# Causal mask by selects, a stream of row maxima and a scaled split of w_out in a transformer layer

## The chip, the cores and the metric

The kernel runs on one core of one Trainium2 chip. The metric is device time in microseconds (us) of one execution, lower being better. The chip's engines are named TensorE (PE), VectorE (DVE), ScalarE (ACT), GpSimd (POOL) and SyncE (SP, which issues most of the DMAs). PEld is TensorE's weight load, which runs beside the matmuls.

## What is computed

One layer for 2048 tokens of width 1024: a token mixer of eight attention heads with forget gates beside a chunked spatial gating unit, one output projection, then a SwiGLU feed-forward block (FFN). The part that the change touches is the attention and what feeds it:

```python
xn = rms_norm(x, mix_norm_g)
q, k, v, f_logit, z = split(xn @ w_in)
c = cumsum(log_sigmoid(f_logit + b_f))          # per head, along the tokens
s = einsum('bqhd,bkhd->bhqk', q, k) * Dh ** -0.5
s = s + c[t] - c[s]
s = where(key_pos <= q_pos, s, -inf)            # causal
p = softmax(s)
attn = einsum('bhqk,bkhd->bqhd', p, v)
...
merged = concatenate([rms_norm(attn, g_a), rms_norm(sgu, g_s)])
x = x + merged @ w_out
```

## The kernel before

All matrix products are made from fp32 numbers that are split in two parts, high and low; a product is three matmuls (high by high, high by low, low by high). `hi_of` casts the high part, `lo_of` subtracts it from the number for the low one; both are helpers, so their instructions carry L102 and L107 wherever they are called.

**Stage 1 (0 to 360 us).** Four chunks of 512 tokens. Each chunk makes the forget gates' rows, q and k, then v, and in between works off pieces of three side jobs through `between`: the rows of the forget gates (`forget_rows`), the next chunk's normalisation and split (`Chunk.steps`), and the row maxima of the previous chunk (`early_max`). A row maximum is the bound that exp subtracts; it needs a product q k of its own with high parts alone (`one_max`, one matmul of up to 512 columns and one reduction on VectorE, 128 queries by 512 keys each), a split of the result (`max_split`) and a transposition (`max_rows`). Everything that the attention reads (QH, QL, KH, KL, VD, XS, the gates' rows AUG) is stored to DRAM through SP's queue. In chunk 0, v is made first, in four PSUM banks that are closed (`v_close`) into normalised tiles after the weights of q have been split.

**Stage 2 (360 to 1011 us).** Attention, over 32 units (head h, chunk of queries j), each of 4j+4 steps of 128 keys: 320 steps. A step is `qk`: two matmuls into PSUM (L624, L625), on the last four steps of a unit, the diagonal blocks, a third (L627) that adds -1e30 above the diagonal by a product of the identity with a mask; then exp on ScalarE into Pt (L629), its cast Ph on ScalarE and its low part Pl on VectorE. Two steps later follows `pv_of`: three matmuls with Ph and Pl (L640 to L642). Between the steps come pieces of the z projections and of the spatial gating (`gates`, up to step 293), of `prep` (loads of the keys two units ahead, and, for the heads and chunks that stage 1 has not covered, their row maxima in one run of 4(j+1) matmuls), and from step 276 on of `out_weights`: w_out is loaded, multiplied by the output gain on GpSimd (`gain`, L799), cast on ScalarE and subtracted on GpSimd. From step 300 on the output tiles follow.

**Stage 3 (1011 to 2511 us).** The FFN; the change doesn't touch it.

Which instruction of an engine comes first is set by a scheduler when the kernel is built: it follows the order of the program, save that an instruction may move ahead of others that are not ready by its model of the engines. Each engine then runs its own list strictly in order, and SP's list of DMAs too. A wait for one tile so holds everything behind it on that engine.

## Time and profile before

| | us |
|---|---|
| median of 3 runs | 2509.7 |
| lowest, highest | 2504.14, 2510.0 |
| profiled execution | 2512.58 |
| its span | 2510.8 |
| TensorE busy | 2437.3 |
| VectorE busy | 1562.2 |
| ScalarE busy | 1054.5 |
| GpSimd busy | 555.6 |

The durations of the profile come from the one profiled execution. Its time has some 1.8 us around the span, and lies 2.9 us above the median of the runs. The busy shares are averages over stages that are unlike, so the profile is read by stretches: a window's row gives each engine's busy time with its number of instructions, and the granted TensorE clock as a share of the full one. Matmuls are pipelined: their records overlap, and the distance from one start to the next, not the length of a record, is what one costs.

### The profile page before, as it was taken

Reading aid. Unit: us, or ns where it says so; the run is one execution under the profiler, and the core shown is the slowest. Engines: PE = TensorE matmul, PEld = TensorE weight load, DVE = VectorE, ACT = ScalarE, POOL = GpSimd, SP = SyncE. Lnnn points to the kernel's source line nnn. Section 1 sums busy time; section 2 is a strip of 40 time slices with the busy share of each in tenths; the row PEclk is TensorE's granted clock in tenths of the full one; section 3 lists DMA queues with packets and bytes.
Section 4 is the critical chain, followed back from the end, with each engine's and each line's share of the span. In section 5 each row is a group of like instructions: output and inputs, shape, how many; then the busy total and the mean of one; then the engine's idle time right before and its main releaser. Section 6 shows DMA issues by size and latency. Waiting matters only on the chain. (4 is left out here: it accounts for less than half of the span.)

```text
span 2510.8 us, 31035 instructions
## 1 busy us (share of the span) xinstructions
PE 2437.3 (97%) x10857; PEld 1949.1 (78%) x10857; DVE 1562.2 (62%) x2537; ACT 1054.5 (42%) x1787; POOL 555.6 (22%) x442
## 2 busy tenths in 40 slices
PE   7899999999999989999999999999999999999998
PEld 5677777787777776877788888878888877888876
DVE  4457485555456666455755555775555587586887
ACT  4312236667777666333423333433232342232333
POOL 1000000000000024122223323233232234454441
PEclk9999999999999988999999999999999999999999
DMA  9766574334433336665422232342322335455454
GB/s 307 259 223 207 162 210 131 93 99 108 112 95 96 89 88 171 187 207 174 159 84 85 84 93 68 93 142 76 93 68 84 93 109 193 168 180 187 134 189 150
DMA packets 351646, 348.25 MB, mean 139 GB/s; under 512 B 54428, under 2 KB 275092, under 8 KB 350466
## 3 DMA queue, kind: packets, MB, share of 16 engines
q1 hardware_dynamic: 349186, 337.88, 43.5%
q0 software_dynamic: 2304, 8.39, 1.1%
q8 instruction: 86, 1.41, 0.2%
q14 instruction: 70, 0.57, 0.1%
HBM read 229.47 MB, written 116.72 MB: 138 GB/s over the span
## 5 line engine op out<-in xcount | busy, mean ns | idle before, releaser
L102 ACT CAST wh<-raw 128x512 fp32r<-128x512 f32 (+2 forms) x500 | 309.3, 624 | 803.0 <-PE pp L1296 648.3
L107 DVE TENSOR_TENSOR wl<-raw,wh 128x512 fp32r<-128x512 f32 (+2 forms) x500 | 371.6, 752 | 116.5 <-ACT wh L102 115.2
L107 DVE TENSOR_TENSOR Pl<-Pt,Ph 128x512 fp32r<-128x512 f32 (+1 forms) x320 | 201.3, 635 | 198.0 <-ACT Ph L102 190.2
L1027 POOL TENSOR_TENSOR raw<-raw 128x512 f32<-128x512 f32 (+1 forms) x124 | 166.3, 1342 | 542.3 <-DMA raw<-in_w_gu_dram 374.1
L629 ACT ACTIVATE Pt<-st 128x512 f32<-128x512 f32 (+1 forms) x320 | 168.4, 532 | 157.0 <-PE st L625 83.3
L672 PE MATMUL z<-wh,xz 128*128 128x512 f32 x512 | 201.6, 403 | 0.0
L102 ACT CAST Ph<-Pt 128x512 fp32r<-128x512 f32 (+1 forms) x320 | 176.2, 556 | 13.5 <-DVE Pl L107 2.4
L1027 DVE TENSOR_TENSOR raw<-raw,raw 128x512 f32<-128x512 f32 (+1 forms) x112 | 133.4, 1192 | 73.1 <-POOL raw L1027 69.2
L339 DVE TENSOR_REDUCE mx<-mx_ps 128x1 f32<-128x512 f32 x192 | 127.9, 685 | 29.2 <-PE mx_ps L337 28.1
L642 PE MATMUL pv<-Pl,V 128*128 128x512 f32 (+1 forms) x320 | 121.9, 381 | 11.2 <-DVE Pl L107 11.2
L337 PE MATMUL mx_ps<-D,A 72*128 72x512 f32 (+5 forms) x320 | 121.8, 402 | 11.3 <-DVE mx L339 5.9
L624 PE MATMUL st<-A,D 74*128 74x512 f32 (+1 forms) x320 | 121.5, 380 | 1.8 <-ACT Pt L629 1.7
L640 PE MATMUL pv<-Ph,V 128*128 128x512 f32 (+1 forms) x320 | 122.7, 383 | 0.4 <-ACT Ph L102 0.3
L625 PE MATMUL st<-B,C 128*128 128x512 f32 (+1 forms) x320 | 119.7, 374 | 0.0
L641 PE MATMUL pv<-Ph,V 128*64 128x512 f32 (+1 forms) x320 | 117.0, 366 | 0.0
L672 PEld LDWEIGHTS z<-wh,xz 128*128 128x128 f32 x512 | 96.7, 189 | 18.9
L1296 PE MATMUL pp<-R2h,wh 128*128 128x512 f32 x264 | 105.2, 398 | 4.9 <-ACT u L1085 4.9
L1296 PE MATMUL pp<-R3h,wl 128*128 128x512 f32 x264 | 104.3, 395 | 2.6 <-DVE wl L107 2.6
L1296 PE MATMUL pp<-R2h,wl 128*128 128x512 f32 x264 | 105.0, 398 | 0.2 <-DVE wl L107 0.2
L1296 PE MATMUL pp<-R1h,wl 128*128 128x512 f32 x264 | 104.4, 395 | 0.7 <-DVE wl L107 0.7
L1296 PE MATMUL pp<-R2l,wh 128*128 128x512 f32 x264 | 104.5, 396 | 0.0
L1296 PE MATMUL pp<-R5h,wh 128*128 128x512 f32 x264 | 104.4, 395 | 0.0
(338 smaller groups left out, 6203.0 us busy)
## 6 DMA issues: line engine op xcount, KB each, us to landing
raw<-in_w_gu_dram SPq DMA_DIRECT2D x88, 512.0 KB
HD<-hT SPq DMA_DIRECT2D x44, 512.0 KB
xz<-XS SPq DMA_DIRECT2D x32, 512.0 KB
XA<-xa SPq DMA_DIRECT2D x27, 512.0 KB
xa<-XA SPq DMA_DIRECT2D x24, 512.0 KB
raw<-HD SPq DMA_DIRECT2D x24, 512.0 KB
xb<-XA SPq DMA_DIRECT2D x24, 512.0 KB
XA<-xb SPq DMA_DIRECT2D x21, 512.0 KB
```

Source lines behind the costliest of these rows:

```text
L102: nc.scalar.copy(o, i)
L107: eng.tensor_tensor(o, i, f(h), ALU.subtract)
L337: nc.tensor.matmul(pm[:, 0:n], lhs, Dt[0 : lhs.shape[0], 0:n], start=True, stop=True)
L339: nc.vector.tensor_reduce(mx[:, a, s : s + 1], pm, AX.X, ALU.max)
L624: nc.tensor.matmul(st[:, off:], Dt[:, b * P : (b + 1) * P], A[:, off:], start=True, stop=False)
L625: nc.tensor.matmul(st[:, off:], C[:, b * P : (b + 1) * P], B[:, off:], start=False, stop=kb < 4 * j)
L629: nc.scalar.activation(Pt[:, off:], st[:, off:], AF.Exp)
L640: nc.tensor.matmul(pv[:, off:], V[:, 0:P], Ph[:, off:], start=kb == 0, stop=False)
L642: nc.tensor.matmul(pv[:, off:], V[:, 0:P], Pl[:, off:], start=False, stop=kb == 4 * j + 3)
L672: nc.tensor.matmul(pz, xz[:, a, k, :], w[b][:, k, :], start=n == 0, stop=n == 3 * KT - 1)
L1027: (nc.vector if e == "v" else nc.gpsimd).tensor_tensor(o, a, b, op)
L1296: nc.tensor.matmul(pm, a[:, k, :], b[:, k, :], start=on is None and k == 0 and e == 0, stop=k == it.kh - 1 and e == 2, skip_group_check=n ...
```

## The change

- The mask: the 128 matmuls of L627 and their two constants go. Instead, after Ph and Pl of a diagonal block are made, two GpSimd selects set the part above the diagonal of each to zero, in place, 128 by 128 each. Pl is made from Pt and Ph, so Ph's select waits for Pl; the pv matmuls wait for both selects.
- The row maxima: `early_max` becomes `max_stream`, which serves stage 1 as before, and in stage 2 makes the maxima of all units that stage 1 left over, in one stream spread evenly over the steps, with its own loads (A and D of 66 rows, pool p2m) in place of the attention's tiles of 72 rows.
- w_out: the gain is the scale of ScalarE's cast, and the low part is one scalar_tensor_tensor on VectorE; GpSimd has no part in it.
- The weights of q are loaded and split in halves, the second half behind `v_close`. `forget_rows` yields three times in place of once for the first two chunks. The stores XS of chunk 0 move from chunk 0 to chunk 1. The splits of w_zu and the constants of the spatial gating (`z_consts`) move into the first z projection.

```diff
 ZEND = 293
+LEND = 276
 ORATE = 2
...
     dmask = T(csm, [P, CH], F32, "dmask")
-    idr = T(csm, [P, P], F32R, "idr")
-    kmask = T(csm, [P, P], F32R, "kmask")
...
         ld(dmask, c_mat[:, 768:1280])
-        nc.vector.tensor_copy(idr, ident)
-        nc.vector.tensor_scalar(kmask, tri, -1.0, -NEG, ALU.add, ALU.mult)
...
         nc.vector.scalar_tensor_tensor(lf, F, 0.0, ln, ALU.min, ALU.subtract)
-        yield
+        for _ in range(3 if j < 2 else 1):
+            yield
         pl = T(ps1, [P, 4, P], F32, "tp")
...
-    def early_max(j):
-        jobs = [(h, s) for h in range(HE[j]) for s in range(j + 1)]
+    def max_stream(units, pl, ps, pp, nd, ahead):
+
+        jobs = [(h, j, s) for h, j in units for s in range(j + 1)]
         As, Ds = {}, {}
...
             if n < len(jobs):
-                h, s = jobs[n]
+                h, j, s = jobs[n]
                 pr, o = h // 2, (h % 2) * DH
                 if s == 0:
-                    A = As[h] = T(p1, [66, CH], F32R, "A")
+                    A = As[h, j] = T(pl, [66, CH], F32R, "A", bufs=2)
                     ldr(A[0:64], QH[pr][j][o : o + DH])
                     ldr(A[64:66], CR[0:2])
-                Dt = Ds[n] = T(p1, [66, CH], F32R, "D", bufs=ND)
+                Dt = Ds[n] = T(pl, [66, CH], F32R, "D", bufs=nd)
                 ldr(Dt[0:64], KH[pr][s][o : o + DH])
...
-        late = None
-        PF = j + 1
-        for n in range(PF):
+        def turn():
+            max_rows(pp, T(ps, [P, 4, P], F32, "mx_ps" if ps is ps2_[0] else "tp", **kw), *late)
+
+        late, kw = None, {"bufs": NMX} if ps is ps2_[0] else {}
+        for n in range(ahead):
             get(n)
-        for n, (h, s) in enumerate(jobs):
-            get(n + PF)
+        for n, (h, j, s) in enumerate(jobs):
+            get(n + ahead)
             if s == 0:
-                mx = T(p1, [P, 4, 4], F32, "mx")
+                mx = T(pp, [P, 4, 4], F32, "mx")
             for a in range(4):
-                one_max(ps1, p1, a, j, s, As[h][:, a * P : (a + 1) * P], Ds[n], mx)
+                one_max(ps, pp, a, j, s, As[h, j][:, a * P : (a + 1) * P], Ds[n], mx)
                 yield
                 if a == 2 and late is not None:
-                    max_rows(p1, T(ps1, [P, 4, P], F32, "tp"), *late)
+                    turn()
                     late = None
             if s == j:
-                late = (h, j, max_split(p1, j, mx))
+                late = (h, j, max_split(pp, j, mx))
         yield
-        max_rows(p1, T(ps1, [P, 4, P], F32, "tp"), *late)
+        turn()
         yield
...
-    nxt = Chunk(0)
+    nxt = first = Chunk(0)
     still = T(p1, [P, CH], F32R, "D", bufs=ND)
...
     nc.vector.tensor_tensor(wf[:, :, 32:40], wfr, f(wf[:, :, 0:8]), ALU.subtract)
-    wq = whole(wgt, w_in[:, 0:512], "w")
+    wq, get_q, halves_q = weight(wgt, w_in[:, 0:512], "w")
+    for i in range(2):
+        get_q(i)
+        halves_q(i)
     load_mats()
...
         v_close(pms[tt], nxt, tt)
+    for i in range(2, 4):
+        get_q(i)
+        halves_q(i)
     wk = whole(wgt, w_in[:, 512:1024], "w")
...
                         n += 1
+                if c == 1 and which == 0:
+                    first.keep(pr)
                 qh = T(p1, [P, CH], F32R, "qh")
...
                 if c == 0:
-                    if which == 0:
-                        xc.keep(pr)
                     qs = T(p1, [P, CH], F32, "D", bufs=ND)
...
                 pass
-        early = early_max(c) if c < NCH - 1 else iter(())
-    for i in range(4):
-        if i > 1:
-            get_u(i)
-        halves_u(i)
-
+        early = max_stream([(h, c) for h in range(HE[c])], p1, ps1, p1, ND, c + 1) if c < NCH - 1 else iter(())
     st1.close()
...
     p2z = pool(stz, "p2z", bufs=2)
+    p2m = pool(stz, "p2m", bufs=2)
     psz = pool(stz, "psz", bufs=2, space=PSUM)
...
         res[h, j] = (A, B)
-        if (h, j) not in MD:
-            mx = T(p2, [P, 4, 4], F32, "mx")
-            for a in range(4):
-                for s in range(j + 1):
-                    one_max(ps2, p2, a, j, s, A[0:72, a * P : (a + 1) * P], kd[h, s][1], mx)
-                    yield
-            mh = max_split(p2, j, mx)
-            yield
-            yield
-            max_rows(p2, T(ps2, [P, 4, P], F32, "mx_ps", bufs=NMX), h, j, mh)
-        ldr(A[72:74], MD[h, j].rearrange("(r b) t -> r (b t)", r=2))
-        yield
+        if (h, j) in MD:
+            ldr(A[72:74], MD[h, j].rearrange("(r b) t -> r (b t)", r=2))
+        else:
+            due.append((h, j))
+
+    def max_due(u):
+
+        if u in due:
+            due.remove(u)
+            while u not in MD:
+                next(lm)
+            ldr(ab[u][0][72:74], MD[u].rearrange("(r b) t -> r (b t)", r=2))
...
         nc.tensor.matmul(st[:, off:], Dt[:, b * P : (b + 1) * P], A[:, off:], start=True, stop=False)
-        nc.tensor.matmul(st[:, off:], C[:, b * P : (b + 1) * P], B[:, off:], start=False, stop=kb < 4 * j)
-        if kb >= 4 * j:
-            nc.tensor.matmul(st[:, off : off + P], idr, kmask, start=False, stop=True)
+        nc.tensor.matmul(st[:, off:], C[:, b * P : (b + 1) * P], B[:, off:], start=False, stop=True)
         Pt = T(p2h, [P, CH], F32, "Pt", bufs=NPT)
...
         lo_of(nc.vector, Pl[:, off:], Pt[:, off:], Ph[:, off:])
+        if kb >= 4 * j:
+
+            for t in (Ph, Pl):
+                d = t[:, off : off + P]
+                nc.gpsimd.affine_select(d, d, [[1, P]], ALU.is_ge, 0.0, base=0, channel_multiplier=-1)
         live[h, j][1].append((V[:, b, :], Ph, Pl, off))
...
+    ZC = {}
+
+    def z_consts():
+        wsr = T(p2z, [P, 8, P], F32, "zr", bufs=2)
+        ld(wsr, w_st.rearrange("g j i -> j g i"))
+        bsc = T(p2z, [P, 8], F32, "bsc", bufs=1)
+        ld(bsc, b_st)
+        lngb = T(p2z, [P, 512], F32, "lngb", bufs=1)
+        ld(lngb, ln_g.rearrange("(o n) -> o n", o=1).broadcast_to([P, 512]))
+        lnbb = T(p2z, [P, 512], F32, "lnbb", bufs=1)
+        ld(lnbb, ln_b.rearrange("(o n) -> o n", o=1).broadcast_to([P, 512]))
+        ZC.update(bsc=bsc, lngb=lngb, lnbb=lnbb)
+        yield
+        nc.vector.memset(wsr[64:128, :, 0:64], 0.0)
+        hi_of(nc.scalar, wst_h, wsr)
+        lo_of(nc.vector, wst_l, wsr, wst_h)
+        yield
+
     def z_proj(i, res):
...
                         n += 1
+                    if i == cc == 0 and (g, k) in ((1, 2), (0, 4)):
+                        next(zc)
+                    if i == cc == 0 and g and k in (0, 1, 4, 5):
+                        n_u = (0, 1, 4, 5).index(k)
+                        halves_u(n_u)
+                        if n_u < 2:
+                            get_u(n_u + 2)
                     yield
...
-        def gain(e):
-            if e < 2 * len(jobs):
-                n, i = divmod(e, 2)
-                kh, fh, pr = jobs[n]
-                k = kh * 4 + pr * 2 + i
-                r = raw[n][:, i, :]
-                nc.gpsimd.tensor_tensor(r, r, E["onc"][:, k : k + 1].broadcast_to([P, CH]), ALU.mult)
-
         get(0)
...
         yield
-        gain(0)
-        yield
         for e in range(2 * len(jobs)):
...
             kh, fh, pr = jobs[n]
-            gain(e + 1)
+            g = E["onc"][:, kh * 4 + pr * 2 + i : kh * 4 + pr * 2 + i + 1]
             if e % 4 == 0:
...
             h_, l_ = (w[:, pr * 2 + i, :] for w in W[kh, fh])
-            hi_of(nc.scalar, h_, raw[n][:, i, :])
-            lo_of(nc.gpsimd, l_, raw[n][:, i, :], h_)
+            nc.scalar.activation(h_, raw[n][:, i, :], AF.Copy, scale=g)
+            nc.vector.scalar_tensor_tensor(l_, raw[n][:, i, :], g, f(h_), ALU.mult, ALU.subtract)
             if i:
...
-    ab = {}
+    ab, due = {}, []
     AHEAD = 2
...
         for u in units[:AHEAD]:
-            for _ in prep(*u, ab):
-                pass
-    wsr = T(p2z, [P, 8, P], F32, "zr", bufs=2)
-    ld(wsr, w_st.rearrange("g j i -> j g i"))
-    nc.vector.memset(wsr[64:128, :, 0:64], 0.0)
-    hi_of(nc.scalar, wst_h, wsr)
-    lo_of(nc.vector, wst_l, wsr, wst_h)
...
+            prep(*u, ab)
+    zc = z_consts()
     zg = gates()
...
     fins = []
-    pg, p_total, p_done = iter(()), 0, 0
+    rest = [u for u in units if u[1] == NCH - 1 or u[0] >= HE[u[1]]]
+    lm, l_total, l_done = max_stream(rest, p2m, ps2, p2, 2, 1), sum(4 * j + 4 for _, j in rest) + 2, 0
     for n in range(len(steps) + DEPTH):
...
             h, j, kb = steps[n]
-            if kb == 0:
-                for _ in pg:
-                    pass
-                ui = units.index((h, j)) + AHEAD
-                if ui < len(units):
-                    pg, p_done = prep(*units[ui], ab), 0
-                    p_total = 4 * (units[ui][1] + 1) + 3 if units[ui] not in MD else 1
-                else:
-                    pg, p_total = iter(()), 0
+            if kb == 0 and units.index((h, j)) + AHEAD < len(units):
+                prep(*units[units.index((h, j)) + AHEAD], ab)
+            max_due(steps[min(n + 3, len(steps) - 1)][0:2])
             qk(h, j, kb)
-            while p_done < p_total * (kb + 1) / (4 * j + 4):
-                next(pg, None)
-                p_done += 1
+            while l_done < l_total * (n + 12) / LEND:
+                next(lm, None)
+                l_done += 1
             while z_done < z_total * n / ZEND:```

How the change moves instructions on the engines, at the places that the prediction speaks of. A row is the line, the operation, what it writes and reads (with the program's running numbers) and its shape.

At the start, ScalarE before: two further casts of w_q's pieces (raw_340, raw_344) stand ahead of the tiles xh of the normalised v.

```order
L102 CAST wh_330<-raw_336 128x1024
L260 ACTIVATE jk_319,ss_239<-xl_311 128x1024
L260 ACTIVATE jk_321,ss_239<-xl_313 128x1024
L102 CAST wh_330<-raw_340 128x1024
L102 CAST wh_330<-raw_344 128x1024
L428 ACTIVATE xh_460<-mm_353,r_2_64 128x8x64
```

ScalarE after, the same place:

```order
L103 CAST wh_328<-raw_334 128x1024
L257 ACTIVATE jk_317,ss_237<-xl_309 128x1024
L257 ACTIVATE jk_319,ss_237<-xl_311 128x1024
L103 CAST wh_328<-raw_464 128x1024
L103 CAST wh_328<-raw_468 128x1024
L429 ACTIVATE xh_448<-mm_341,r_2_64 128x8x64
```

The rows stand in the same order; the two casts now read tiles that are asked for later (raw_464, raw_468).

On TensorE in chunk 0's q, before: the transposition of the forget gates (L311, tile v) stands ahead of the four of the next chunk's r (L270), near the end of the third q product (mm_662).

```order
L509 MATMUL mm_662<-xh_234,wh_330 128x512
L509 MATMUL mm_662<-xl_238,wh_330 128x512
L311 MATMUL tp_633<-ident_63,v_574 128x128
L270 MATMUL tp_644<-ident_63,r_2_64 128x128 x4
L509 MATMUL mm_662<-xh_234,wl_331 128x512
```

After: those of r stand behind the first matmul of the third product (mm_650), and that of the forget gates comes later.

```order
L516 MATMUL mm_592<-xl_236,wh_328 128x512
L516 MATMUL mm_592<-xh_232,wl_329 128x512
L516 MATMUL mm_650<-xh_229,wh_328 128x512
L267 MATMUL tp_632<-ident_63,r_2_64 128x128 x4
L516 MATMUL mm_650<-xl_233,wh_328 128x512
```

The transpositions of r moved 19 matmuls forward.

TensorE at the first unit of the attention, before (st is the product q k, pv the product with v):

```order
L624 MATMUL st_3414<-A_3355,D_3350 128x384
L625 MATMUL st_3414<-B_3358,C_3347 128x384
L627 MATMUL st_3414<-kmask_68,idr_67 128x128
L624 MATMUL st_3432<-A_3355,D_3350 128x256
L625 MATMUL st_3432<-B_3358,C_3347 128x256
L627 MATMUL st_3432<-kmask_68,idr_67 128x128
L624 MATMUL st_3448<-A_3355,D_3350 128x128
L625 MATMUL st_3448<-B_3358,C_3347 128x128
L640 MATMUL pv_3388<-Ph_3395,V_884_3337 128x512
```

After:

```order
L627 MATMUL st_3428<-A_3342,D_3337 128x384
L628 MATMUL st_3428<-B_3345,C_3334 128x384
L627 MATMUL st_3451<-A_3342,D_3337 128x256
L628 MATMUL st_3451<-B_3345,C_3334 128x256
L627 MATMUL st_3478<-A_3342,D_3337 128x128
L628 MATMUL st_3478<-B_3345,C_3334 128x128
L627 MATMUL st_3521<-A_3357,D_3337 128x512
L646 MATMUL pv_3379<-Ph_3385,V_880_3324 128x512
```

The mask matmuls are gone, and the pv of the first block stands behind four qk of this unit and the first matmul of the next.

GpSimd at the same place, before: the clearing of three V tiles, then the products of w_out's first pieces.

```order
L574 MEMSET V_886_3339 128x4x64
L574 MEMSET V_887_3340 128x4x64
L574 MEMSET V_888_3341 128x4x64
L799 TENSOR_TENSOR xa_9447<-xa_9447,onc_9445 128x512 x2
L799 TENSOR_TENSOR xa_9449<-xa_9449,onc_9445 128x512 x2
```

After:

```order
L577 MEMSET V_884_3328 128x4x64
L639 AFFINE_SELECT Ph_3385<-Ph_3385 128x128
L639 AFFINE_SELECT Pl_3387<-Pl_3387 128x128
L639 AFFINE_SELECT Ph_3433<-Ph_3433 128x128
L639 AFFINE_SELECT Pl_3435<-Pl_3435 128x128
```

Six more pairs follow without another instruction between: GpSimd's list is now mostly selects up to the end of the attention.

VectorE in the end stretch, before: Pl, the reductions of a unit two ahead, and the spatial gating (sg).

```order
L107 TENSOR_TENSOR Pl_9765<-Pt_9761,Ph_9763 128x512
L339 TENSOR_REDUCE mx_9644<-mx_ps_9767 128x1
L342 ISA jk_9772,mx_9644<-mx_ps_9770,dmask_66 128x384
L342 ISA mx_9644 128x1
L656 RECIPROCAL sr_9747<-sr_9747 128x32
L107 TENSOR_TENSOR Pl_9793<-Pt_9789,Ph_9791 128x384
L339 TENSOR_REDUCE mx_9644<-mx_ps_9795 128x1
```

After, in the last units too:

```order
L108 TENSOR_TENSOR Pl_9996<-Pt_9992,Ph_9994 128x512
L740 SCALAR_TENSOR_TENSOR sg_9884<-z_9885,bsc_3497,zr_9124 128x2x64 x2
L836 SCALAR_TENSOR_TENSOR R2l_10010<-xa_9933,onc_9828,R2h_10009 128x512 x2
L108 TENSOR_TENSOR Pl_10020<-Pt_10016,Ph_10018 128x512
L108 TENSOR_TENSOR Pl_10043<-Pt_10039,Ph_10041 128x512
L836 SCALAR_TENSOR_TENSOR R2l_10010<-xa_9987,onc_9828,R2h_10009 128x512
```

The scaled subtractions of w_out (L836) stand where the reductions stood.

## Rows read from the trace of the kernel before

**Rows 1.** The page's engines: busy us, share of the span, instructions.
```profile
PE 2437.3 (97%) x10857; PEld 1949.1 (78%) x10857; DVE 1562.2 (62%) x2537; ACT 1054.5 (42%) x1787; POOL 555.6 (22%) x442
```
**Rows 2.** Stretches: length, busy PE, PEld, DVE, ACT, POOL, granted clock, DMA share, GB/s.
```profile
395.00:914.00 519.00, 512.56 (x2513) 410.23 (x2512) 291.11 (x607) 361.89 (x664) 16.69 (x18) 1.00 0.37 101
914.00:976.00 62.00, 51.50 (x199) 39.11 (x198) 49.61 (x93) 41.77 (x81) 36.62 (x30) 0.75 0.39 118
```
**Rows 3.** Waits of TensorE, 0 to 100 us: us in total, times, longest.
```profile
PE tp L311 <- DVE v L308: 9.2, 1, 9.2
PE mm L482 <- DVE xh L429: 6.3, 1, 6.3
```
**Rows 4.** Timeline, ScalarE near 63 us: start, length, instruction, idle before it.
```profile
62.98 1.06 ACT L260 ACTIVATE jk<-xt 128x1024 bf16<-128x1024 f32 x1 [3.17 <-DMA xt<-in_x_dram]
```
**Rows 5.** Waits of TensorE, 100 to 160 us.
```profile
PE mx_ps L337 <- DVE mx L342: 3.2, 3, 1.7
```
**Rows 6.** Timeline, VectorE near 141 us.
```profile
140.97 1.23 DVE L241 TENSOR_TENSOR xt<-xt,rb 128x1024 f32<-128x1024 f32 x1 [2.07 <-DMA xt<-in_x_t_dram]
```
**Rows 7.** Waits of TensorE, 360 to 395 us.
```profile
PE pv L642 <- DVE Pl L107: 3.5, 1, 3.5
```
**Rows 8.** Timeline, VectorE near 371 us.
```profile
370.58 0.48 DVE L934 MEMSET zr<- 64x512 f32 x1 [4.59 <-DMA zr<-in_w_st_dram]
```
**Rows 9.** Waits of TensorE, 395 to 914 us.
```profile
PE pv L642 <- DVE Pl L107: 3.9, 7, 0.8
```
**Rows 10.** Groups, 914 to 976 us: busy, mean ns | idle before, releasers.
```profile
L337 PE MATMUL mx_ps<-D,A 72*128 72x512 f32 (+3 forms) x28 | 14.0, 520 | 4.1 <-DVE mx L339 2.1 <-DVE mx L342 1.9
L799 POOL TENSOR_TENSOR xa<-xa,onc 128x512 f32<-128x512 f32 x12 | 13.7, 1166 | 0.7 <-DMA xa<-in_w_out_dram 0.7
L339 DVE TENSOR_REDUCE mx<-mx_ps 128x1 f32<-128x512 f32 x20 | 13.2, 681 | 4.8 <-PE mx_ps L337 4.6
...
L102 ACT CAST R0h<-xa 128x512 fp32r<-128x512 f32 x4 | 2.5, 613 | 0.0
```
**Rows 11.** Line 627: duration ns min/median/max, first and last start us.
```profile
L627 PE MATMUL st<-kmask,idr x128: 220/223/308, 361.0 to 1019.7; 128*128 128x128 f32 x128
```
**Rows 12.** Timeline, TensorE at two mask matmuls.
```profile
361.02 0.22 PE L627 MATMUL st<-kmask,idr 128*128 128x128 f32 x1
361.08 0.41 PE L624 MATMUL st<-A,D 74*128 74x384 f32 x1
...
601.01 0.27 PE L627 MATMUL st<-kmask,idr 128*128 128x128 f32 x1
601.12 0.44 PE L672 MATMUL z<-wh,xz 128*128 128x512 f32 x1
```
**Rows 13.** Groups of the whole run, small GpSimd operations: busy, mean ns.
```profile
L847 POOL TENSOR_TENSOR sq<-sq 128x128 f32<-128x128 f32 x16 | 8.8, 550 | 1.2
...
L574 POOL MEMSET V<- 128x256 f32 x3 | 0.9, 324 | 7.2 <-PE mx_ps L337 7.2
```
**Rows 14.** Timeline, a diagonal block near 670 us: VectorE, then TensorE.
```profile
668.50 0.69 DVE L107 TENSOR_TENSOR Pl<-Pt,Ph 128x512 fp32r<-128x512 f32 x1 [1.25 <-ACT Ph L102]
...
671.97 0.45 PE L640 MATMUL pv<-Ph,V 128*128 128x512 f32 x1
672.26 0.40 PE L641 MATMUL pv<-Ph,V 128*64 128x512 f32 x1
672.49 0.39 PE L642 MATMUL pv<-Pl,V 128*128 128x512 f32 x1
```
**Rows 15.** Timeline, VectorE: the cast of 128x4 at 319 and 938 us.
```profile
319.04 0.16 DVE L349 CAST mh<-m 128x4 fp32r<-128x4 f32 x1
...
937.78 1.23 DVE L349 CAST mh<-m 128x4 fp32r<-128x4 f32 x1
```
**Rows 16.** Timeline, GpSimd near 938 us.
```profile
937.37 2.83 POOL L107 TENSOR_TENSOR R2l<-xa,R2h 128x512 fp32r<-128x512 f32 x2
```
**Rows 17.** Line 246, a scaled cast on ScalarE: duration ns min/median/max.
```profile
L246 ACT ACTIVATE xh<-xt,mixc x24: 706/722/728, 72.7 to 253.0; 128x512 fp32r<-128x512 f32 x24
```

More of the change, by code (lines that the diff above doesn't have):

```diff
@@ L689, in z_proj @@
             zv = zr[:, cc, 512:1024]
-            nc.vector.scalar_tensor_tensor(zv, zv, mv[:, cc, 0:1], lngb, ALU.subtract, ALU.mult)
-            nc.vector.scalar_tensor_tensor(zv, zv, rv[:, cc : cc + 1], lnbb, ALU.mult, ALU.add)
+            nc.vector.scalar_tensor_tensor(zv, zv, mv[:, cc, 0:1], ZC["lngb"], ALU.subtract, ALU.mult)
+            nc.vector.scalar_tensor_tensor(zv, zv, rv[:, cc : cc + 1], ZC["lnbb"], ALU.mult, ALU.add)
             zv8 = zv.rearrange("p (g d) -> p g d", g=8)
```

8 lines of the change are left out of this document (1 added, 7 removed).

## The prediction

> **What bounds the kernel now.** The engine line comes first: TensorE is busy 2437.3 us, 97% of the span [rows 1]. An edit therefore pays in two ways only: it takes matmuls away where TensorE never pauses, or it shortens a stretch in which TensorE waits or runs at the lower clock. Next comes the table by stretches, to see which is which. In the middle of the attention (395 to 914 us) TensorE is busy 512.56 of 519 us at granted clock 1.00, so at most 6.4 us of waiting can be won there [rows 2]. The end of the attention (914 to 976) is another kind: TensorE 51.5 of 62 us at a clock of 0.75, VectorE 49.61, ScalarE 41.77, GpSimd 36.62, so no engine is full [rows 2]. Nothing of the 1500 us of FFN behind it is touched.
>
> Then the waits of TensorE, stretch by stretch. In the first 100 us it waits 9.2 us at L311 and 6.3 us for the normalised v (tile xh) [rows 3]; near the first, ScalarE takes the square of the next chunk's rows at 62.98, having waited 3.17 us for their load [rows 4]. In chunk 1 it waits 3.2 us for maxima [rows 5], since VectorE sat behind a late load of x_t and has 1.23 us pieces queued ahead [rows 6]. At the start of the attention one wait of 3.5 us for Pl stands out [rows 7]: VectorE's clearing of the z constants waited 4.59 us for their DMA, with Pl behind it [rows 8]. In the middle, Pl costs 3.9 us over 7 waits [rows 9]. At the end, the groups show the crowd: 28 max matmuls (14.0 us, 4.1 of idle before them), 20 full-width reductions on VectorE (13.2 us), products and subtractions for w_out on GpSimd [rows 10].
>
> **The mask matmuls.** 128 of them go [rows 11]. Their 223 ns is no price: matmuls overlap, and what one costs is the distance to the next start. That is 0.06 us at 361.02 and 0.11 us at 601.01 [rows 12]. I take the middle, 0.085, as neither row is more typical: 128 x 0.085 = 10.9 us, ends 7.7 and 14.1. Some 12 lie in the end stretch, where TensorE is not full, so I count 116: **-10 us** (-7 to -14).
>
> **The selects.** 256 go to GpSimd, two to a diagonal block, one after the other on one queue. The trace has no select. Its nearest rows are a 128x128 tensor_tensor at 550 ns and a 128x256 memset at 324 ns [rows 13]. A select reads one operand and writes one, so it lies between the two; I take 0.5, ends 0.3 and 1.2 (a contended 128x512 product, in [rows 10], as the far end). Cover: in a typical diagonal block Pl begins at 668.50 and takes 0.69, and the pv matmul on Ph starts at 671.97, 2.8 us after Pl's end [rows 14]. Two selects at 0.5 fit in it twice over. In the built order too the pv of a block stands two steps behind its qk, with z and max matmuls between. The select of Ph has to wait for VectorE's subtraction, which reads Ph whole, so both selects lie behind Pl: the pv matmul on Ph becomes as late as the one on Pl. Blocks that have short cover, four to each of the first two units and those after the z work has run out, are priced with their stretches below.
>
> The other cost is on VectorE. While GpSimd does two subtractions (2.83 us from 937.37), VectorE's cast of 128x4 takes 1.23 us, against 0.16 with GpSimd idle [rows 15, 16]. The Trainium skill (SBUF — State Buffer, Who interferes with whom) says why: the two engines share a port pair under an exclusive lock, and a VectorE instruction with two SBUF inputs is held by a GpSimd instruction that reads SBUF. This speaks against the change, since each select reads SBUF; the trace agrees in size (1.23 beside 0.16). In a sum from the rows, a select of 0.5 can hold VectorE for 0.5 us, 1 us for each diagonal block, in the middle of some 2 us of step (32 units of ten steps on average in the 658.6 us between the first and last mask matmul, [rows 11]). VectorE keeps idle time there (291.11 of 519 busy, [rows 2]), so I charge little.
>
> **The streamed maxima.** The same matmuls and reductions, 66 rows deep instead of 72, now evenly spread and done by step 264 rather than in bunches of 12 to 16 two units ahead. In the middle this can take away part of the 3.9 us of Pl waits [rows 9] and adds 28 matmuls that move in from the end (priced there). For the selects' lock and late Ph against the smoother maxima I take **+1 us** (-4 to +6, the lower end being two thirds of the 6.4 us of idle, the upper as much again lost).
>
> **The end stretch.** The 28 max matmuls at 0.23 us (the step from 672.26 to 672.49, [rows 14]) cost 6.4 us where they arrive. Here their reductions go (13.2 us and the masked ones). GpSimd loses all 16 products (1.17 us each) and 16 subtractions; VectorE gets 16 scaled subtractions instead, at about the 0.69 of a 128x512 subtraction, 11 us; ScalarE's 16 casts (613 ns) become scaled casts (722 ns, [rows 10, 17]), +1.7 us, without waiting for GpSimd. VectorE ends at 49.61 - 13.2 + 11 = 47.4 or less, since the masked reductions and GpSimd's company go too. ScalarE, at 41.77 + 1.7 = 43.5, is a floor that nothing lowers. How much of its 20.2 idle us stays is not in any row: I leave a third, since exp still waits for qk and the clock may fall again. 43.5 + 6.7 = 50 us instead of 62: -12 here, +6.4 in the middle, net **-5.5 us** (-12 at the floor with nothing lost elsewhere, +3 if the length stays and four late units pay for their selects).
>
> **Start of the kernel.** The w_q pieces 2 and 3 move behind v_close in the program, but in the order as built both their casts still stand ahead of v_close's rows on ScalarE, so the 6.3 us wait stays [rows 3]. L311 moves back behind some 28 further matmuls, but the transposes of the next chunk's r now stand 19 matmuls earlier, and r is there only after the square at 62.98 [rows 4]: the 9.2 us wait becomes a wait for r of about the same end. **0** (-4, if the XS stores moved out let x arrive sooner, to +3). **Chunk 1:** its x_t load now stands ahead of the AUG store on SP: most of the 3.2 us goes, **-2.5** (0 to -4). **Start of the attention:** the clearing of the z constants leaves the head of VectorE's queue, which frees the 3.5 us [rows 7, 8]. What comes in its place: eight selects in a row on GpSimd within the first eight diagonal blocks (4 us at 0.5) with nothing but qk between, the streamed maxima's D and A loads and xz queued on SP, the later w_z halves. I take **+2** (-2 to +4).
>
> **Sum.** -10 + 1 - 5.5 + 0 - 2.5 + 2 = -15 us against the profiled execution (2512.58, itself 1.8 above its span): 2497.6. That execution is 2.9 above the median of the three runs, so on the median's scale **2495 us**, own range 2488 to 2502.
>
> **Rivals.**
> A. The forecast. For it: TensorE full in the middle, cover of 2.8 us; chance 0.53.
> B. Only the mask's gain stays. The end keeps its length because ScalarE and the waits for qk, not the max work, set it (ScalarE's gap there is filled by waiting for TensorE at half clock), the start gives 4 us back to the selects. -10 + 1 + 1.5 (end) + 0 - 1 + 4 = -4.5 us, 2505. For it: 41.77 us of ScalarE against a clock of 0.75. Against: 4.1 us of idle stand before the max matmuls themselves [rows 10]. 0.21.
> C. Slower: the selects outrun their cover. Place: the four diagonal blocks at a unit's end, eight selects on one queue, with pv and everything behind it on TensorE waiting. A step lasts 2 us and holds two selects, so the point is 1.0 us each; above it the queue grows by what is over, eight times a unit. At 1.1, with the lock on VectorE included, that is 8 x 0.1 + 0.1 = 0.9 us a unit, 32 units: +29 us, against the other -15 (+1 taken out: -16): 2512.6 + 13 - 2.9 = 2523. For it: GpSimd products measure 1.17 us where both engines work [rows 10]. Against: those are four times as wide; the 128x128 row has 550 ns [rows 13]. The rule of the skill named above would act in just this way. 0.12.
> D. More is won: the end at ScalarE's floor (-12), the start at -2, the middle at -4, chunk 1 and mask as in A: -10 - 12 - 2 - 4 - 2.5 = -30.5, but hardly all together; I put 26 us, 2484. For it: the 10.5 us that TensorE idles at the end [rows 2] and a clock that stays up once it does not. 0.14.
>
> **How the numbers follow.** The likeliest is A, 2495. The range leaves out most of C and the outer third of D: 2482 to 2511. About 0.3%, 7.5 us, is what a measurement can tell from no change: faster is under 2502.2 (A almost whole, D: 0.65), the same up to 2517.2 (B, the edges of A and C: 0.22), slower 0.13.
>
> **What the profile of the changed kernel would show.** Right: 128 matmuls fewer in the engine line; selects of 0.3 to 0.6 us; in the waits, pv for Ph or Pl below 8 us in the middle, with GpSimd named for few; the stretch from the last full steps to the first out tiles near 50 us, at a higher clock than 0.75, with ScalarE busiest; no wait of 3 us for Pl at the start. Wrong: selects over 1 us, or pv matmuls that wait for GpSimd in every unit (C); an end stretch of 60 us with ScalarE waiting for qk (B); TensorE's middle longer than its matmuls by more than 10 us; new waits for r or for XS loads in the first 400 us.

## The result and the profile after

The changed kernel takes 2479.2 us (median of 4 runs), against 2508.0 for the kernel before: a ratio of 0.9887, 95% interval 0.9869 to 0.9905, 28.8 us faster. The forecast was 15 us (2495, range 2482 to 2511): the sign was right, the gain nearly twice the size, and the time lies below the range. Rival D, 2484 at a chance of 0.14, came nearest. The medians here and below leave out two executions that took several times as long as all others (9137 us of the kernel before, 10293 us of hybrid_again).

The engine line of the changed kernel, which answers to [rows 1]; TensorE has lost its 128 mask matmuls, GpSimd has gained 256 selects and lost 32 operations on w_out:

```profile
PE 2415.8 (97%) x10729; PEld 1930.5 (78%) x10729; DVE 1568.5 (63%) x2551; ACT 1054.0 (43%) x1787; POOL 596.7 (24%) x666
```

Windows at fixed times compare different work, so from here the stretches are cut where the first qk matmul of a step starts: steps 0 to 20 of the attention, 20 to 279, 279 to 300, 300 to 319. The columns are those of [rows 2]. The kernel before:

```profile
360.47:405.39 44.92, 39.70 (x175) 30.74 (x174) 24.60 (x47) 25.55 (x47) 2.04 (x2) 0.92 0.67 177
405.39:912.97 507.58, 501.36 (x2463) 401.57 (x2462) 286.06 (x598) 354.10 (x650) 14.66 (x16) 1.00 0.37 99
912.97:971.43 58.46, 47.96 (x180) 36.14 (x179) 46.44 (x88) 37.86 (x72) 36.62 (x30) 0.74 0.35 108
971.43:1019.52 48.09, 46.71 (x217) 36.00 (x215) 28.23 (x48) 29.10 (x56) 8.61 (x12) 1.00 0.70 193
```

The changed kernel:

```profile
356.20:396.00 39.80, 37.09 (x163) 28.90 (x162) 25.77 (x49) 25.02 (x46) 4.59 (x16) 0.96 0.69 193
396.00:894.81 498.81, 493.67 (x2394) 395.30 (x2393) 306.32 (x641) 352.95 (x651) 75.40 (x218) 1.00 0.42 116
894.81:937.64 42.83, 34.10 (x139) 24.79 (x137) 30.30 (x58) 37.05 (x70) 10.29 (x22) 0.80 0.51 149
937.64:986.83 49.19, 47.19 (x213) 35.92 (x211) 30.01 (x50) 30.09 (x58) 13.47 (x26) 1.00 0.70 187
```

So 5.1 us go at the attention's start, 8.8 in its middle, 15.6 in the end stretch, and 1.1 come back behind it. Some 4 us less stand ahead of the first step (360.47 against 356.20). A stretch differs between executions of one program: in three executions of the changed kernel the first 20 steps took 39.8, 42.7 and 39.7 us, the middle 498.8, 499.4 and 502.2, the end stretch 42.8, 42.8 and 43.3. In the end stretch ScalarE, with 37.05 of 42.83 us, is now the busiest engine; VectorE fell from 46.44 to 30.30.

The waits of TensorE in the changed kernel, by the same stretches (start, middle, end), which answer to [rows 7, 9] (us in total, times, longest):

```profile
PE st L627 <- ACT Pt L630: 2.4, 2, 1.6
...
PE pv L646 <- POOL Ph L639: 2.7, 6, 0.8
PE pv L646 <- ACT Ph L103: 0.8, 2, 0.4
...
PE pv L646 <- POOL Ph L639: 5.7, 3, 4.4
PE pv L646 <- ACT Ph L103: 1.7, 4, 0.8
```

The 3.5 us wait for Pl at the start is gone; in the middle and at the end, TensorE now waits most for the selects of Ph. Their durations by form, ns (min/median/max):

```profile
L639 POOL TENSOR_SCALAR_AFFINE_SELECT Ph<-Ph x128: 289/294/796, 360.6 to 988.4; 128x128 fp32r<-128x128 f32 x128
L639 POOL TENSOR_SCALAR_AFFINE_SELECT Pl<-Pl x128: 289/295/740, 361.1 to 988.6; 128x128 fp32r<-128x128 f32 x128
```

The longest wait at the end carries GpSimd's name but isn't its doing. TensorE, GpSimd and ScalarE there (timelines):

```profile
902.58 0.80 PE L646 MATMUL pv<-Ph,V 128*128 128x512 f32 x1 [4.39 <-POOL Ph L639]
...
902.23 0.29 POOL L639 TENSOR_SCALAR_AFFINE_SELECT Ph<-Ph 128x128 fp32r<-128x128 f32 x1 [5.46 <-DVE Pl L108]
...
897.64 1.28 ACT L710 ACT_TABLE_LOAD   x1
898.94 1.91 ACT L710 ACTIVATE zr<-zr 128x2048 f32<-128x2048 f32 x1
900.75 0.60 ACT L103 CAST Ph<-Pt 128x512 fp32r<-128x512 f32 x1
```

GpSimd waited 5.46 us for Pl, Pl for the cast Ph, and that cast stood behind a table load of 1.28 us and the 1.91 us GELU on ScalarE: the chain starts on ScalarE. The kernel with mask matmuls in place of the selects (mask_back_again, below) has nearly the same wait there, under ScalarE's name:

```profile
905.80 0.58 PE L632 MATMUL st<-A,D 74*128 74x256 f32 x1 [4.28 <-ACT Pt L637]
```

### The profile page after: what moved, and what is told of

Read it like the earlier page. It is cut to its first block, busy times and chain, and to the rows that moved or that the text cites. A ratio compares the mean times of both kernels' runs of the same rounds, so it can differ in the third digit from the quotient of the medians.

```text
span 2479.6 us, 31430 instructions
## 1 busy us (share of the span) xinstructions
PE 2415.8 (97%) x10729; PEld 1930.5 (78%) x10729; DVE 1568.5 (63%) x2551; ACT 1054.0 (43%) x1787; POOL 596.7 (24%) x666
## 5 line engine op out<-in xcount | busy, mean ns | idle before, releaser
L103 ACT CAST wh<-raw 128x512 fp32r<-128x512 f32 (+2 forms) x500 | 309.6, 624 | 796.5 <-PE pp L1300 657.4
L108 DVE TENSOR_TENSOR wl<-raw,wh 128x512 fp32r<-128x512 f32 (+2 forms) x500 | 374.6, 758 | 116.2 <-ACT wh L103 115.8
L108 DVE TENSOR_TENSOR Pl<-Pt,Ph 128x512 fp32r<-128x512 f32 (+1 forms) x320 | 194.5, 615 | 158.8 <-ACT Ph L103 155.0
L630 ACT ACTIVATE Pt<-st 128x512 f32<-128x512 f32 (+1 forms) x320 | 167.9, 534 | 149.9 <-PE st L628 148.6
L103 ACT CAST Ph<-Pt 128x512 fp32r<-128x512 f32 (+1 forms) x320 | 176.2, 557 | 22.6 <-PE pv L647 6.2
L337 DVE TENSOR_REDUCE mx<-mx_ps 128x1 f32<-128x512 f32 x192 | 130.8, 686 | 37.6 <-PE mx_ps L335 35.1
L646 PE MATMUL pv<-Ph,V 128*128 128x512 f32 (+2 forms) x320 | 123.6, 387 | 11.7 <-POOL Ph L639 8.8
L639 POOL TENSOR_SCALAR_AFFINE_SELECT Ph<-Ph 128x128 fp32r<-128x128 f32 x128 | 44.2, 345 | 374.7 <-DVE Pl L108 255.0
L627 PE MATMUL st<-A,D 74*128 74x512 f32 (+1 forms) x320 | 120.7, 378 | 3.8 <-ACT Pt L630 3.8
L335 PE MATMUL mx_ps<-D,A 66*128 66x512 f32 (+2 forms) x320 | 118.5, 382 | 4.8 <-DVE mx L337 3.7
L628 PE MATMUL st<-B,C 128*128 128x512 f32 (+1 forms) x320 | 118.3, 370 | 0.0
L1146 POOL TENSOR_TENSOR hT<-hT 128x512 f32<-128x512 f32 x44 | 74.4, 1693 | 127.3 <-DVE hT L1145 104.2
```

Of the source, the lines that this page charges most:

```text
L103: nc.scalar.copy(o, i)
L108: eng.tensor_tensor(o, i, f(h), ALU.subtract)
L335: nc.tensor.matmul(pm[:, 0:n], lhs, Dt[0 : lhs.shape[0], 0:n], start=True, stop=True)
L337: nc.vector.tensor_reduce(mx[:, a, s : s + 1], pm, AX.X, ALU.max)
L627: nc.tensor.matmul(st[:, off:], Dt[:, b * P : (b + 1) * P], A[:, off:], start=True, stop=False)
L628: nc.tensor.matmul(st[:, off:], C[:, b * P : (b + 1) * P], B[:, off:], start=False, stop=True)
```

## The experiments

Medians with the ratio to the kernel before on the same chip:

| kernel | us | ratio, 95% interval |
|---|---|---|
| mask_alone | 2509.7 | 1.0011 (1.0001 to 1.0020) |
| stream_alone | 2499.0 | 0.9966 (0.9954 to 0.9979) |
| wout_alone | 2505.2 | 0.9995 (0.9984 to 1.0006) |
| zmove_alone | 2506.7 | 0.9997 (0.9988 to 1.0006) |
| mask_back | 2479.7 | 0.9888 (0.9874 to 0.9903) |
| stream_back | 2507.8 | 1.0007 (0.9997 to 1.0017) |
| wout_back | 2490.1 | 0.9935 (0.9918 to 0.9952) |
| no_select | 2473.1 | 0.9861 (0.9847 to 0.9876) |
| stream_wout | 2487.2 | 0.9920 (0.9908 to 0.9933) |
| after_again | 2478.9 | 0.9886 (0.9872 to 0.9900) |
| mask_back_again | 2479.6 | 0.9895 (0.9881 to 0.9910) |
| one_select | 2478.7 | 0.9885 (0.9871 to 0.9899) |
| hybrid | 2474.4 | 0.9868 (0.9855 to 0.9882) |
| startup_back | 2478.2 | 0.9887 (0.9868 to 0.9905) |
| zmove_back | 2480.5 | 0.9893 (0.9876 to 0.9911) |
| both_back | 2483.7 | 0.9906 (0.9891 to 0.9921) |
| after_third | 2480.8 | 0.9892 (0.9877 to 0.9907) |
| hybrid_again | 2479.6 | 0.9882 (0.9862 to 0.9902) |

**One part alone.** Each is the kernel before with one part of the change. The diffs show the lines that matter; `...` stands for lines left out.

mask_alone, the mask part:

```diff
-            nc.tensor.matmul(st[:, off : off + P], idr, kmask, start=False, stop=True)
...
+            for t in (Ph, Pl):
+                d = t[:, off : off + P]
+                nc.gpsimd.affine_select(d, d, [[1, P]], ALU.is_ge, 0.0, base=0, channel_multiplier=-1)
```

> The kernel before with the mask part alone: the 128 mask matmuls go, 256 GpSimd selects come; maxima, w_out and the start as before. Theory P (the price by start distances, 0.06 to 0.11 us each, is right, and the selects are covered): 9 to 11 us faster, 2498, with the saving spread over the steps and nothing else moved. Theory M (a mask matmul cost more than its own start distance, since the matmul behind it and exp also wait): 15 us or more faster, 2493. If the selects do not fit under their cover in this order: less than 5 us, with TensorE waiting for GpSimd in most units.

It gives nothing (2.1 us slower on the medians): neither theory; the time is that of the third case. Middle and end stretch:

```profile
404.89:907.99 503.10, 491.17 (x2359) 388.87 (x2358) 287.31 (x598) 352.56 (x650) 76.72 (x220) 1.00 0.36 100
907.99:968.55 60.56, 50.12 (x172) 36.14 (x171) 42.18 (x87) 38.08 (x72) 42.82 (x50) 0.66 0.36 106
```

and TensorE's waits for selects in both:

```profile
PE pv L638 <- POOL Ph L631: 7.4, 9, 2.8
...
PE pv L638 <- POOL Ph L631: 6.9, 5, 2.0
```

The middle gains 4.5 us net of 7.4 us of waits for selects, which are 9, about one in three of its units, where the case had said most; the end stretch, where the selects share GpSimd's list with w_out, is 2.1 us longer, at a granted clock of 0.66 against 0.74.

stream_alone, the maxima (`lm` is max_stream, spread over the steps; `pg` was `prep` with its own maxima):

```diff
-                next(pg, None)
...
+                next(lm, None)
```

> The kernel before with the stream of row maxima alone; mask matmuls, GpSimd's w_out and the start as before. Theory S (the bunches of maxima cost the middle spacing between matmuls and crowd the end): 12 us or more faster, about 5 of it in the middle although 28 max matmuls (6 us) move into it, and 8 to 10 at the steps 279 to 300. Theory C (the maxima were only crowded at the end by GpSimd's w_out work): under 5 us, the end still over 53 us long because VectorE and GpSimd hold each other up.

wout_alone, the split of w_out:

```diff
-            hi_of(nc.scalar, h_, raw[n][:, i, :])
-            lo_of(nc.gpsimd, l_, raw[n][:, i, :], h_)
+            nc.scalar.activation(h_, raw[n][:, i, :], AF.Copy, scale=g)
+            nc.vector.scalar_tensor_tensor(l_, raw[n][:, i, :], g, f(h_), ALU.mult, ALU.subtract)
```

> The kernel before with w_out alone changed (gain as the scale of ScalarE's cast, subtraction on VectorE), maxima and mask as before. Theory C (GpSimd's w_out work held VectorE up at the end): 6 to 10 us faster, the steps 279 to 300 shorter than 52 us. Theory S (the maxima did it): within 3 us of before, since VectorE now has the 16 subtractions (11 us) beside the maxima and is the bound of that stretch.

stream_wout, both of these diffs together:

> The kernel before with two parts, the stream of maxima and w_out; mask matmuls, the constants' place and the start as before. Alone these parts gave 8.6 and 2.4 us. Theory E (each of the two still leaves the other's work as the bound of the end stretch, and only both together clear it; the steps 279 to 300 were 58.5 us before, 50.1 and 52.0 with one part, 41.2 with all but the mask): 2486 to 2490, the stretch at 41 to 43 us. Theory Z (the missing 16 us of the whole come from the start and the moved constants): 2495 to 2498, the stretch over 46.

The end stretch of stream_alone, of wout_alone and of stream_wout, one kernel each:

```profile
908.32:958.39 50.07, 35.52 (x150) 25.93 (x148) 30.72 (x43) 36.37 (x71) 37.92 (x30) 0.83 0.44 137
```

```profile
908.27:960.31 52.04, 41.83 (x181) 31.73 (x179) 44.92 (x102) 38.07 (x70) 1.76 (x2) 0.87 0.36 105
```

```profile
904.54:947.71 43.17, 35.59 (x147) 26.35 (x146) 29.58 (x58) 36.90 (x70) 1.76 (x2) 0.80 0.46 145
```

With the stream alone GpSimd stays at 37.92 us; with w_out alone VectorE stays at 44.92 of 52.04. With both, ScalarE's 36.9 is the most, at 43.17 us, where 58.46 was before. In this stretch the two gains add up: 8.4 and 6.4 us alone, 15.3 together. In the next stretch (300 to 319) each part by itself loses some of it again (49.3 and 51.3 us, against 48.1 before), both together lose nothing (48.0). On the medians, against 2507.6 and 2506.3 for the kernel before on the two chips, 8.6 and 2.4 us alone become 19.0 together. The time and the length of the stretch are those that theory E gave, but its reason, that only both clear the end stretch, isn't what the stretch shows: of the 8.0 us that the two win beyond their sum, the profiles show 4.5 in the stretch behind it, and the rest isn't located. What ScalarE waited for in the kernel before (timeline):

```profile
931.20 0.62 ACT L102 CAST R2h<-xa 128x512 fp32r<-128x512 f32 x1 [2.38 <-POOL xa L799]
```

The middle of stream_alone:

```profile
402.73:908.32 505.59, 502.58 (x2497) 407.33 (x2495) 304.96 (x641) 355.12 (x651) 18.26 (x18) 1.00 0.41 114
```

It holds 34 matmuls more than the 2463 of before and is 2.0 us shorter. By the distances from start to start in the two traces, 28 more maxima take 5.5 us more (29.9 to 35.4), and the other matmuls 7.8 us less (477.8 to 470.0), of which 4.0 us had been idle time before them: the bunches had cost the middle more than the arriving maxima cost.

zmove_alone, the constants and the w_zu splits moved into the first z projection:

> The kernel before with only the splits of w_zu and the constants of the spatial gating moved into the first z projection. If the 3.5 us wait for Pl behind the clearing of the constants and the lower clock after it are what the attention's start lost: 4 to 6 us faster, all of it in the first 20 steps. If another load only takes its place on SP's queue: within 2 us.

0.9 us on the medians, within the noise, so the second case; the first 20 steps took 42.0 us in its profile, against 44.9.

**One part undone.** Each is the changed kernel with one part as before.

mask_back and, beside the changed kernel (after_again) on one chip, mask_back_again:

```diff
-                nc.gpsimd.affine_select(d, d, [[1, P]], ALU.is_ge, 0.0, base=0, channel_multiplier=-1)
...
+            nc.tensor.matmul(st[:, off : off + P], idr, kmask, start=False, stop=True)
```

> The changed kernel with the mask matmuls back in place of the selects; stream, w_out and the rest as changed. On the kernel before, the mask part alone gave nothing. Theory I (the stream of maxima is what makes room for the selects, so that beside it the matmuls' whole price is won): 8 to 11 us slower than the changed kernel, 2488 to 2490. Theory N (the mask part gives nothing anywhere and the other parts carry the gain): within 2 us of the changed kernel, 2479.

> The changed kernel once more, on the chip and in the rounds of the mask's comparison: 2477 to 2481, the difference to the next run being what counts.

> The changed kernel with the mask matmuls in place of the selects, on the same chip. If the mask part gives nothing (theory N): within 2 us of the changed kernel; if it gives the half that a saving of 7 us in the middle less 3 at the end suggests: 3 to 5 us slower.

no_select, which leaves the causal mask out altogether:

```diff
-                nc.gpsimd.affine_select(d, d, [[1, P]], ALU.is_ge, 0.0, base=0, channel_multiplier=-1)
```

> The changed kernel without the 256 selects: the causal mask is left out, so the time is that of the kernel with a free mask. If the selects are covered beside the stream (theory I): 2 to 5 us faster, 2474 to 2477, about the waits for them that the profile names. If they hold VectorE up as well (shared port): 10 us or more faster, 2469, with VectorE's Pl subtractions shorter in the middle.

Middle and end stretch of mask_back_again, then of after_again, then of no_select:

```profile
392.28:898.17 505.89, 502.79 (x2496) 407.19 (x2495) 304.83 (x641) 354.60 (x651) 13.35 (x14) 1.00 0.41 114
898.17:938.93 40.76, 32.43 (x148) 22.50 (x147) 29.40 (x58) 36.81 (x70) 1.76 (x2) 0.92 0.50 153
```

```profile
396.64:896.08 499.44, 494.00 (x2394) 395.33 (x2392) 306.32 (x641) 352.82 (x651) 75.62 (x218) 1.00 0.42 115
896.08:938.90 42.82, 34.35 (x138) 24.95 (x137) 30.33 (x58) 37.04 (x70) 10.27 (x22) 0.80 0.48 148
```

```profile
394.64:887.72 493.08, 490.37 (x2394) 395.37 (x2393) 304.39 (x641) 353.20 (x651) 13.89 (x14) 1.00 0.43 117
887.72:932.90 45.18, 36.40 (x138) 26.18 (x137) 30.32 (x60) 38.15 (x72) 1.78 (x2) 0.77 0.52 153
```

The mask part is worth 0.7 us on one chip, nothing that can be told from zero: theory N. A free mask would be worth some 6.5 us (2479.7 to 2473.1, on one chip). In the middle, 103 matmuls less make 12.8 us (505.89 to 493.08, one profile of each), 0.124 us each, and the selects take 6.4 of that back, of which only 2.7 us show as waits for them. VectorE's busy time hardly differs (306.3 against 304.4), which speaks against selects that hold VectorE up. The reverse is in the traces: a select can be held while VectorE runs subtractions of two operands back to back. The longest one in a third execution of the changed kernel (after_third), GpSimd and then VectorE:

```profile
771.23 2.42 POOL L639 TENSOR_SCALAR_AFFINE_SELECT Ph<-Ph 128x128 fp32r<-128x128 f32 x1 [1.79 <-DVE Pl L108]
...
770.81 0.89 DVE L108 TENSOR_TENSOR Pl<-Pt,Ph 128x128 fp32r<-128x128 f32 x2
771.62 1.29 DVE L108 TENSOR_TENSOR zvl<-zr,zvh 128x512 fp32r<-128x512 f32 x2
772.82 0.69 DVE L108 TENSOR_TENSOR Pl<-Pt,Ph 128x512 fp32r<-128x512 f32 x1
```

The subtractions keep their 0.69 us, the select takes 2.42 in place of 0.29 and ends 0.15 us after the last of them, and TensorE waits 2.59 us for it. The middle of that execution took 502.24 us, so over three executions the selects' price there is 6 to 9 us, and the mask part's net gain in the middle 4 to 7. How the part that no wait names comes about isn't settled.

The stretch behind the end gives 1.2 us back (48.0 to 49.2, in each of three executions). The 2 us of the end stretch (40.76 to 42.82) can't be put down to the selects: no_select took 45.18 us there, at a clock of 0.77 (0.80 and 0.92 in the two others).

stream_back, the maxima in bunches again:

> The changed kernel with the maxima in bunches again (made two units ahead, as before); selects, w_out and the rest as changed. Theory I (selects need the stream): 15 to 20 us slower than the changed kernel, 2494 to 2499, with TensorE waiting for the selects of Ph for 7 us or more in the middle and at the end. Theory W (the selects' partner is w_out leaving GpSimd): under 10 us slower, 2487 to 2489, about the 8.6 that the stream gave alone.

Theory I and more: 28.6 us slower than the changed kernel, all of the gain. The middle has 7.4 us of waits for selects of Ph, the end stretch 4.1. Its end stretch:

```profile
904.43:964.79 60.36, 52.98 (x172) 39.20 (x170) 45.93 (x102) 38.55 (x70) 9.89 (x22) 0.63 0.32 93
```

It is longer than that of wout_alone (52.04), which has the same maxima but mask matmuls. VectorE's work is about the same in both (45.93 and 44.92 us), and TensorE is busy for longer (52.98 against 41.83) with fewer matmuls, at a granted clock of 0.63 against 0.87: the difference is matmuls at the lower clock, not waits, of which it has fewer (7.2 us in all against 10.0). What holds the clock down there isn't shown.

wout_back, w_out on GpSimd again:

> The changed kernel with w_out's gain and subtraction on GpSimd again. Theory I: little in the middle; at the end, the selects stand behind products and subtractions of 1.2 to 1.4 us on GpSimd's list, so the steps 279 to 300 become 8 to 12 us longer, 2488 to 2491. Theory W (w_out leaving GpSimd is what lets the selects run everywhere): also the middle longer, by 5 us or more. If neither: within 3 us, 2480.

As theory I: the middle is unchanged (498.7), the end stretch grows to

```profile
896.01:949.09 53.08, 39.60 (x141) 28.70 (x140) 30.02 (x43) 36.65 (x71) 44.61 (x50) 0.71 0.46 131
```

with GpSimd, 44.61 us, the busiest engine.

startup_back, zmove_back and both_back (with after_third beside it) undo the start's move, the constants' move, and both:

> The changed kernel with the start as before: w_q split whole ahead of v, one yield in the forget gates' rows, XS of chunk 0 stored in chunk 0; the constants' move stays. Forecast's step (the start is worth 0): within 2 us of the changed kernel, 2477 to 2481. If the 8 us between the kernel with stream and w_out alone (2487.2) and the one with all but the mask (2479.6) lie in the start: 3 to 5 us slower, in the first 100 us.

> The changed kernel with the w_zu splits and the constants of the spatial gating ahead of the attention again. If their place is worth what the first 20 steps show (42.8 us with stream and w_out alone, 38.5 to 39.2 with all but the mask): 4 to 6 us slower than the changed kernel, 2483 to 2485. If the forecast's +2 for that stretch was right (other loads and selects take their place): within 2 us.

> The changed kernel with both moves undone, the start's and that of the spatial gating's constants: stream, w_out and selects alone. Each move undone by itself cost -0.7 and +1.6 us. If the two are independent: 2479 to 2481. If either is enough and only losing both costs what stream and w_out alone lack (7.6 us): 2485 to 2488, with the first 20 steps over 42 us and the first 100 us over 99.

> The changed kernel on the chip of the two runs beside it, as their reference: 2477 to 2481.

The start's move is worth nothing (0.7 us faster without it on other chips); the constants' move 1.6 us (2480.5 against 2478.9, also on other chips); both together 3.0 on one chip (2483.7 against 2480.8). That is less than the 7.6 us between stream_wout and mask_back_again, and what fills the difference isn't settled; of the two profiles' difference, 4.4 us lie in the first 20 steps (42.84 and 38.47), 2.4 in the end stretch, 2.2 ahead of the first step. The first 20 steps say more than the medians: with the stream and the constants' move both in, ten of eleven profiles have 38.5 to 40.3 us (after_again 42.7); with the stream and not the move, four have 42.6 to 43.6; with the move and not the stream, two have 42.0 and 44.5; with neither, three have 44.3 to 45.8. So the attention's start is won by stream and move together, some 3 to 4 us of it by the move beside the stream. Added on one chip in this order, the parts give 19.0 us (stream and w_out), 7.6 (the two moves) and 0.7 (the mask); without the moves the mask part gives 3.5 (2487.2 to 2483.7), so the two take from each other, by what the runs don't show.

**Two other kernels.** one_select puts one select on Pt behind exp in place of the two:

```diff
+            d = Pt[:, off : off + P]
+            nc.gpsimd.affine_select(d, d, [[1, P]], ALU.is_ge, 0.0, base=0, channel_multiplier=-1)
```

> The changed kernel with one select per diagonal block, on Pt right behind exp, in place of two on Ph and Pl. The part of a free mask was 6 us (2473). If the selects cost by their work and by standing behind Pl: 2 to 4 us faster than the changed kernel. If one select between exp and the cast holds ScalarE's list up: as fast or slower, 2479 to 2486, with ScalarE's casts waiting for GpSimd.

The same time (2478.7): half the selects, placed earlier in the chain, win nothing. Number and place change at once here, so the run doesn't tell which of the two is the price.

hybrid and hybrid_again keep mask matmuls where cover is short:

```diff
+        by_pe = kb >= 4 * j and (n < 24 or n >= 276)
...
+        if by_pe:
+            nc.tensor.matmul(st[:, off : off + P], idr, kmask, start=False, stop=True)
...
+        if kb >= 4 * j and not by_pe:
```

> The changed kernel with mask matmuls on the diagonal blocks of the first three units (steps 0 to 23) and from step 276 on, and selects between. By the stretches of the two kernels on one chip (steps 20 to 279: 499.5 us with selects, 505.9 with matmuls; steps 0 to 20, 279 to 300 and 300 to 319: 42.7, 42.8, 49.2 against 38.5, 40.8, 48.0), theory G (the gain of the selects in the middle is given back where cover is short): 3 to 6 us faster than the changed kernel, 2473 to 2476. If the give-back is run to run spread of the start and not the selects: 2477 to 2479.

> The mix of mask matmuls (steps 0 to 23 and from 276) and selects, beside the changed kernel on one chip. It gave 2474.4 on another chip. If the give-back at the ends is real: 3 to 5 us faster than the changed kernel; if that was the chip: within 2 us.

The first run looked like a gain of 4.5 us, the second, beside the changed kernel on one chip, shows 1.1. So it isn't shown to beat the changed kernel, and theory G, that the give-back at the ends can be won back so, isn't shown either: its end stretch took 44.3 and 42.8 us in the two profiles, no less than with selects, and the stretch behind it 48.0 in both, as with mask matmuls.

## Why the prediction was wrong

- **The stream of maxima** is the step that failed most. The forecast charged 6.4 us for the 28 matmuls that come into the middle, and let the smoother maxima and the selects make +1 between them. The 28 cost 5.5, near the forecast, but the stream alone made the middle 2.0 us shorter, because the other matmuls won 7.8. The 3.9 us of Pl waits [rows 9] had been read as the most that bunches cost; but the matmuls between also stood further apart, and 3.8 of the 7.8 us weren't idle time that a wait shows.
- **The mask.** 0.085 us a matmul was too little: 0.124 in the middle, above the upper end taken from [rows 12]. As a distance to the next start it was about right (0.073 us on average over the 103 in mask_back_again); leaving the matmul out wins more than that distance. The selects' median, 0.29 us, lay at the lower end of 0.3 to 1.2 (0.5 was taken), but that they are covered was wrong: 6.4 us in the middle. Net -6.4 there (-3.7 with after_third's middle), where 103 x 0.085 less the 1 us for the selects had made -7.8; over the whole, nothing. The lock was expected to hold VectorE, and its row, a cast of 128x4 [rows 15], reads one operand, while the rule that it was put under speaks of two; what the runs show is single selects held by VectorE, up to 2.42 us beside the stream and 2.68 in mask_alone. Rival C had the place, pv waiting for selects, but not the size: it needed over 1 us for all of them, and the queue that it feared, growing through each unit, isn't there.
- **The end stretch** was right in mechanism: the work of VectorE and GpSimd goes, ScalarE becomes the busiest engine. It was sized at -12 and measured -15.6, and the two parts make 8.4 and 6.4 of it. That each of them alone would lose part of it again in the next stretch wasn't in the forecast.
- **The attention's start** had the wrong sign: +2 forecast, -5.1, -2.3 and -5.2 in three executions of the changed kernel. The wait for Pl went [rows 7, 8], as forecast; of what was to take its place, eight selects and late loads, the waits show 0.2 us in two of them and 1.1 in the third, all of it for loads. That the stream would shorten this stretch too wasn't seen.
- **Chunk 1** was a misreading: the 3.2 us wait [rows 5] belonged to that execution. The chunk took 83.2 us there and 79.5 in the changed kernel, so the term of -2.5 seems to come true; but wout_alone, zmove_alone and mask_alone, which leave the chunk as before, took 80.0, 78.6 and 78.8, with 1.8, 0.7 and 0.6 us of that wait. So that is luck. mask_alone has SP's list as before there, the AUG store ahead of the x_t load, and in its waits stands

```profile
PE mx_ps L333 <- DVE mx L338: 0.6, 1, 0.6
```

The issue of that store on SP took 2.03 us in the kernel before and 0.47 us in mask_alone (timelines), and the x_t load behind it was issued at 135.59 and at 134.81; that this difference made the wait is likely, not shown:

```profile
133.51 2.03 SPq L98 DMA_DIRECT2D AUG<-augs  x1
```

```profile
134.29 0.47 SPq L98 DMA_DIRECT2D AUG<-augs  x1
```

- **The start** at 0 was right: the wait at L311 [rows 3] became one for r (changed kernel, waits of the first 100 us), and undoing the move changed nothing that the medians show.

```profile
PE tp L267 <- POOL r L261: 8.9, 2, 6.4
```

The terms that were off, on the scale of the profiled executions: 8.4 us in the maxima, less 1.4 in the mask, 6.4 at the attention's start (3.6 in after_again), against a sum of -0.7 for eight mask matmuls and the +2, 3.6 at the end, less 1.1 behind it. With them the forecast of -15 becomes -31 (-28); the profiled executions lie 31.3 apart, the medians 28.8. That the sum closes says little, since it still holds chunk 1's -2.5, and single stretches differ by 3 us between executions.

## What to carry over

Parts tried alone needn't add up: here 8.6 and 2.4 us made 19.0, and part of what each won in one stretch it lost in the next, so read the stretch behind as well. Matmuls that come in bunches, with reductions behind them, cost more than the waits that the profile names, so compare lengths of equal stretches of work. A wait seen in one execution should be looked for in a second one before it is booked as a gain, and a loss should be looked for in a kernel that lacks its supposed cause.

## What was not expected of the hardware

A 128x128 select on GpSimd takes 0.29 us, less than a 128x128 sum there (0.55, [rows 13]). In the changed kernel's profile 34 of 256 take over 0.4 us, up to 0.80, and each of these had an instruction of VectorE beside it; beside runs of VectorE's two-operand subtractions single ones took 2.42 us (after_third) and 2.68 (mask_alone), while the subtractions kept their 0.69 and 0.67. A mask matmul of 128 columns cost TensorE 0.124 us in the middle, though the next matmul mostly starts after 0.06 to 0.11.
